# A larger fixed part per float32r matmul in the costs of a hand-written list schedule (hybrid decoder block)

## The chip, the cores and the metric

The kernel runs on one core of a Trainium2 chip. The core has TensorE (PE in the profile; its weight loads are a row of their own, PEld), VectorE (DVE), ScalarE (ACT), GpSimd (POOL) and SyncE (SP, which here issues the DMAs). The metric is the device time of one execution in microseconds; what is compared is the median of several runs.

## The reference

One decoder block for 256 tokens of width 1024, in float32. Three token mixers run on the same normalised input: NSA attention with 16 heads in 4 groups (compressed, selected and window keys), an mLSTM with 4 heads, and cross-attention to 256 memory tokens with 4 heads. Gates merge them; an output projection and a SwiGLU channel mixer of width 2816 follow, each with its RMS norms and residual.

```python
def reference(x, mem, ...):
    ...
    h = rmsnorm(x, g_pre_mix[l])
    z = h @ w_in[l]
    q_nsa, kv_nsa, g_nsa, qkv_ml, if_ml, o_ml, q_mem, g_merge = jnp.split(z, offsets, axis=-1)
    ...
    y_nsa = (gb[..., 0:1] * o_cmp + gb[..., 1:2] * o_slc + gb[..., 2:3] * o_win).reshape(B, S, NSA_Q)
    ...
    y_ml = (jax.nn.sigmoid(o_ml.astype(jnp.float32)) * h_ml).astype(x.dtype)
    y_mem = memory_xattn(q_mem, mem, g_mem[l], w_mem_kv[l])
    gm = jax.nn.sigmoid(g_merge.reshape(B, S, N_BRANCH, D_MODEL))
    y = (gm[:, :, 0] * (y_nsa @ w_proj_nsa[l]) + gm[:, :, 1] * (y_ml @ w_proj_ml[l])
         + gm[:, :, 2] * (y_mem @ w_proj_mem[l]))
    x = x + rmsnorm(y @ w_out[l], g_post_mix[l])
    h = rmsnorm(x, g_pre_ffn[l])
    gu = h @ w_ffn_in[l]
    gate, up = gu[..., :D_FF], gu[..., D_FF:]
    x = x + rmsnorm((jax.nn.silu(gate) * up) @ w_ffn_down[l], g_post_ffn[l])
```

## The kernel before

**Products.** A float32 operand is split into two float32r parts, high and low (`split`: ScalarE copies to the high part, VectorE subtracts it from the source). A product is three matmuls: high by high, high by low, low by high (`mm3`). The weights come as 162 units of 128 x 1024 floats. For a unit, SP loads `raw` (4 buffers), ScalarE writes `whi` and VectorE `wlo` (4 buffers each), and TensorE uses it in 24 matmuls of 256 columns (features on the partitions, `fmaj`) or 12 of 512 columns (tokens on the partitions, `tmaj`).

**Stages, in program order.** Keys and values of the memory branch (to about 28 us), the first input projections with compressed keys and the gates (to about 70 us), memory attention and the NSA keys and values (to about 102 us), then NSA attention, interleaved with the rest of the input projections and the mLSTM (to about 295 us), merge (to about 342 us), output projection, channel mixer.

**NSA attention.** `nsa_half` handles one of the 4 groups for one half of the 128 + 128 tokens. It does two pairs of heads. For each head, TensorE makes scores `sc` (one PSUM tile for the first half of the tokens, two for the second; the tag "s" has three buffers), VectorE takes three maxima `mx`, and ScalarE three exponentials with their sums (into `pc` and `pp`). Per pair VectorE normalises, TensorE transposes (`ptn`), ScalarE and VectorE split the result (`pTh`, `pTl`), and TensorE multiplies with the values (`pvn`). After each half, `fill` records some of the other tasks, named by the letters of `ORDER`, as many as `FILL` says.

**The order of the work.** Nothing is issued as it is written. `Plan.record` keeps every instruction with the parts of tiles that it reads and writes. `Plan.cost` (line 228) estimates its duration. `Plan.schedule` (line 265) then plays the program in planned time: on every engine, among the instructions whose inputs are ready and whose tiles have a buffer, the one first in the program is next (`later` moves some back). If nothing early in the program is ready, a later one is taken, so dense products of the tasks stand between the steps of the attention. `Plan.issue` (line 370) issues all instructions in the order of their planned starts, and that is the order of each engine's queue on the chip, the DMA queue of SP included. On the chip an engine takes its queue in order: if its next instruction is not ready, the engine waits, whatever stands behind.

Planned times of the other engines, in ns: ScalarE 50 (source or result in PSUM) or 95, plus 0.833 per element, plus 93 where it also sums or has a per-partition operand; VectorE 67 plus 1.04 per element (0.52 for a few), plus 60 for each per-partition operand. A result is counted as ready for another engine after the producer's latency (PE 257, ACT 202, DVE 188), with 200 more where TensorE is the one that waits (lines 257 to 263).

A matmul's planned cost and weight load (lines 236 to 240):

```python
if op.eng == "PE":
    dtype = op.a[1].dtype
    op.load = 56.0 if dtype == BF16 else 109.0 if dtype == F32R or op.method == "transpose" else 214.0
    rate = 1.2 if op.method == "transpose" else 0.6 if dtype == F32 else 2.4
    return n / rate + 2
```

In the schedule a matmul starts no sooner than the last matmul's start plus its own `load` (line 337), and TensorE is taken again from its start plus its cost. All instructions are issued from line 382, so every row of the profile names that line; groups are told apart by tile.

Of the kernel before, what the change touches and what calls it, by code (L numbers as in the profile page):

```python
# [17 lines left out]
P = 128  # L18
S = 256          # tokens
D = 1024  # L20
KD = D // P      # feature tiles of the model dimension
NH, NG, HPG, DH = 16, 4, 4, 64
# [9 lines left out]

# columns of w_in
C_Q, C_KV, C_G, C_ML, C_IF, C_O, C_QM, C_MG = 0, 1024, 2560, 2608, 4144, 4152, 4664, 5176

# columns of the array of constants
K_ID, K_TRI, K_RV, K_BM, K_M0, K_C1, K_MT, K_END = 0, 128, 256, 257, 261, 533, 549, 677
# columns of the array of gains and small weights
V_PRE, V_MEM, V_PM, V_PF, V_PO, V_CW, V_CB, V_PEK, V_PEV, V_END = 0, 8, 16, 24, 32, 40, 72, 80, 96, 112


# [1 line left out]
class View:  # L43
    """A part of a tile that has no place yet."""

# [53 lines left out]
    def region(self):  # L99
        """First and last partition, and the elements of a partition as bits."""  # L100
        t = self.tile
        key = repr(self.steps)
        if key not in t.regions:
            p = int(self.ix.flat[0]) // t.n
            bits = np.zeros(t.n, bool)
            bits[self.ix[0].ravel() % t.n] = True
            t.regions[key] = (p, p + self.shape[0], int.from_bytes(np.packbits(bits).tobytes(), "big"))
        return t.regions[key]


class Slot:
    """A tile of the plan: its place is chosen when its first instruction is issued."""

# [49 lines left out]
class Plan:  # L163
    """Records the instructions in program order, with what they read and write, and issues them
    in the order of a list schedule: on every engine the ready one that comes first in the
    program. Tiles of a tag get their buffers in program order."""

# [7 lines left out]
    @contextmanager  # L175
    def later(self, n):
        """The instructions inside come as if n places later in the program."""
        self.boost -= n
        yield
        self.boost += n  # L180
# [47 lines left out]
    def cost(op):  # L228
# [7 lines left out]
        if op.eng == "PE":  # L236
            dtype = op.a[1].dtype
            op.load = 56.0 if dtype == BF16 else 109.0 if dtype == F32R or op.method == "transpose" else 214.0
            rate = 1.2 if op.method == "transpose" else 0.6 if dtype == F32 else 2.4
            return n / rate + 2  # L240
        n = max(v.n for v in views)
# [23 lines left out]
    def schedule(self):  # L265
# [10 lines left out]
        def offer(op):  # L276
            """Makes op a candidate if its new tiles can have places; else it waits for the tag."""
            r = op.ready
            for t in op.tiles:
                if t.real is None:  # L280
                    tag = t.tag
                    if tag.next != t.seq or not tag.free:
                        tag.waiting.setdefault(t.seq, []).append(op)
                        return
                    r = max(r, tag.free[0][0])
            avail[op.eng].append((max(r, held(op)), op))

        def held(op):
            """A bank of PSUM serves one engine at a time, and so do the ports that GpSimd shares."""
            ends = [end + self.latency(o, op) for t in op.tiles if t.psum  # L290
                    for e, (o, end) in t.busy.items() if e != op.eng]
            if op.port:
                ends += [end for e, end in port.items() if e != op.eng]
            return max(ends, default=0.0)
# [91 lines left out]
def block_kernel(ctx, tc, order, xN, xT, memT, cst, vec, row, wg, w1, w2, W, out):  # L386
# [16 lines left out]

# [1 line left out]
    cs = one.tile([P, K_M0], F32, name="cs")  # L405
    vc = one.tile([P, V_END], F32, name="vc")
    ident = cs[:, K_ID:K_ID + P]

# [1 line left out]
    def ps_d(shape, name="pd"):  # L410
# [16 lines left out]

# [1 line left out]
    def split(hi, lo, src):  # L429
        ACT.activation(hi, src, AF.Copy)  # L430
        DVE.tensor_sub(lo, src, hi.bitcast(F32))

# [1 line left out]
    ready = {}  # L434
# [27 lines left out]
    def fmaj(out, xs, ks, wu, b0=0, first=True, last=True):  # L462
        """out [128 features, 256] += blocks of a unit (from b0) times the tiles ks of xs."""
        hi, lo = wu
# [5 lines left out]
    def fpair(xs, w, i, ps_new=ps_d):  # L470
        """[128, 2, 256]: the i-th pair of feature tiles of the weights w."""
        ps = ps_new([P, 2, S])
# [4 lines left out]
    def tmaj(xs, *key, n=4, ps_new=ps_d, into=None, last=0):  # L477
        """[128 tokens, 512] for both halves of the tokens, from n units of two feature tiles each; the
        last ones are used for the first half of the tokens before the second."""
        ps = [ps_new([P, 512]) for _ in range(2)]  # L480
# [21 lines left out]

# [1 line left out]
    ones = one.tile([P, P], F32, name="ones")  # L504
# [4 lines left out]
    def warm_up(n):  # L509
        """Products of no use, that bring the tensor engine's clock up while it would wait."""  # L510
        ps = ps_v([P, P], "warm")
# [3 lines left out]
    def colsum(sq):  # L515
        """[128, 2]: per token, the sum of sq [128, 2, 256] over the partitions and the tiles."""
        col = ps_t([P, 2], "col")
# [6 lines left out]
    def bcast(r, ps):  # L524
        """ps [128, 256]: the column r [128, 2] of the tokens, on every row."""
        for tb in range(2):
# [10 lines left out]

# [1 line left out]
    memt = bigt("G", 3, [P, KD, S], F32, "memt")  # L539
# [99 lines left out]
    DVE.tensor_copy(identb, ident)  # L639
    msk = one.tile([P, 416], BF16, name="msk")          # m0 (272), c1 (16), mt (128)  # L640
    DVE.tensor_copy(msk, mraw)
    M0, MC1, MT, MD = msk[:, 0:272], msk[:, 272:288], msk[:, 288:416], msk[:, 0:P]

# [1 line left out]
    w1t = []  # L645
# [25 lines left out]

# [1 line left out]
    pgf = ps_s([P, S], "pgf")  # L673
# [22 lines left out]

    # running sums of logf, and i - sums
    tri = cs[:, K_TRI:K_TRI + P]
# [32 lines left out]

    # columns: selected keys 128-255, 0-127, compressed keys, window keys 0-127, 128-255
    kh = bigt("KK", 2, [P, NG, 528], F32R, "kh")
# [15 lines left out]

# [1 line left out]
    qkm = [bigt("G", 3, [P, 8, S], F32R, f"qkm{i}") for i in range(2)]  # L751
# [21 lines left out]

# [1 line left out]
    on = bigt("C", 1, [P, 2, 1024], F32, "on")  # L775
# [9 lines left out]

# [1 line left out]
    qm = [bigt("qs", 2, [P, 4, S], F32R, f"qm{i}") for i in range(2)]  # L787
# [3 lines left out]

# [1 line left out]
    ymemt = bigt("E", 2, [P, 2, 4, S], F32R, "ymemt")  # L793
    ymem = [ymemt[:, i] for i in range(2)]
    msc = float(P) ** -0.5
    for h2 in range(2):
        pvm = ps_v([P, 2, S], "pvm")
        ptm = [[work.tile([P, 2, S], F32R, tag=f"pT{i}", bufs=2, name="pTm") for i in range(2)] for _ in range(2)]
        for tb in range(2):
# [16 lines left out]
            for hh_ in range(2):  # L816
                DVE.tensor_scalar(p2[:, hh_, :], p2[:, hh_, :], sm[:, hh_:hh_ + 1], None, op0=ALU.mult)
            pt = ps_t([P, 2, 2, P], "ptx")          # m tile, head, t
            for mt in range(2):
# [11 lines left out]

# [1 line left out]
    for br in range(2):  # L833
# [17 lines left out]

# [1 line left out]
    num = on[:, 1, :].rearrange("p (a h d) -> p a h d", a=2, h=4)  # L853
# [65 lines left out]

# [1 line left out]
    gm = [bigt("G", 3, [P, 8, S], F32, f"gm{b}") for b in range(3)]  # L921
# [117 lines left out]

# [1 line left out]
    last_exp = exps[-12:]  # L1041
# [23 lines left out]

# [1 line left out]
    x1 = bigt("C", 1, [P, 2, D], F32, "x1")  # L1067
# [7 lines left out]
    def scaled(name, xs, n, g, z, scale, pre):  # L1075
        """z [128 tokens, 2, 1024]: the products with the units of a name times the gains g and, per token,
        pre; yields per half of the tokens 1/rms of the products times the root of scale."""
        ss = work.tile([P, 2, 2], F32, tag="ss", bufs=2, name="ss")
# [32 lines left out]

# [1 line left out]
    wq = [bigt(tg, n, [P, 2, 1024], F32R, "wq") for tg, n in (("Y", 2), ("Y", 2), ("V", 1), ("E", 2))]  # L1113
# [53 lines left out]
def _layout(inputs):  # L1167
# [8 lines left out]
    units = {}  # L1176

    def blocks(w, cols, k0=0, k1=None):
        """[128, k, cols] of the rows k0..k1 (tiles)."""
        k1 = w.shape[0] // P if k1 is None else k1  # L1180
# [68 lines left out]
def _stream(units, order):  # L1249
    """The units in the order of their use."""  # L1250
    import numpy as np

    return np.stack([units[key] for key in order])
# [24 lines left out]
```

## Time and profile before

| | us |
|---|---|
| median of 3 runs | 562.93 |
| lowest and highest run | 562.88, 563.34 |
| span of the profiled execution | 561.4 |
| ScalarE busy in the span | 334.2 |
| VectorE busy in the span | 404.5 |

The profile is of one execution; its span runs from the first to the last instruction, and no other time of that execution is given. The mean granted TensorE clock was 0.996 of full speed. Matmuls overlap in the records (the next begins while the last still drains), so the spacing of their starts, not their mean duration, is what one costs. In a group's row, the number after "x" is the count, then follow busy time in us, the mean duration in ns, and after the second bar the engine's idle time just before, with what ended it. In the chain of waits each row has start in us, length in us and the run of instructions.

### The profile page before, as it was taken

How to read it: one execution, taken by the hardware profiler on the slowest of the kernel's cores; microseconds unless marked ns; L12 is line 12 of the kernel's file. 1: busy time of each engine (PE TensorE's matmuls, PEld its weight loads, DVE VectorE, ACT ScalarE, POOL GpSimd, SP SyncE). 2: the span in 40 equal slices, each digit the busy share in tenths (PEclk: the TensorE clock that was granted, in tenths of full speed). 3: DMA queues.
4: the chain of work that ended last, by engine and by line, in shares of the span. 5: the costliest groups of instructions: out<-in, count | busy, mean ns of one | idle time of the engine just before them, and what ended most of it. 6: DMA issues, size and time to landing. Idle time of an engine off the chain costs nothing.

```text
span 561.4 us, 10304 instructions
## 1 busy us (share of the span) xinstructions
PE 551.9 (98%) x3964; PEld 516.5 (92%) x3964; DVE 404.5 (72%) x802; ACT 334.2 (60%) x658; POOL 36.0 (6%) x44
## 2 busy tenths in 40 slices
PE   8999999999999999999999999999999999999994
PEld 8899998998989999999999998878999999988883
DVE  4897398598897989987786877865565656654543
ACT  6775677566596858777697444774444444444430
POOL 1110000002002011302111000000000000000000
PEclk9999999999999999999999999999999999999998
DMA  7994327617345253434435655744555545556522
GB/s 246 356 350 154 113 86 228 205 56 238 129 121 180 76 178 124 135 119 160 151 117 158 216 189 188 257 156 123 177 189 183 182 175 179 186 185 191 189 71 75
DMA packets 29281, 95.28 MB, mean 170 GB/s; under 512 B 3376, under 2 KB 6704, under 8 KB 28976
## 3 DMA queue, kind: packets, MB, share of 16 engines
q1 hardware_dynamic: 29232, 94.63, 51.5%
q8 instruction: 31, 0.51, 0.4%
q14 instruction: 18, 0.15, 0.1%
HBM read 92.52 MB, written 1.05 MB: 167 GB/s over the span
## 4 chain that ended last, share of the span: by engine, by line
PE 92%; DMA 3%; ACT 2%; DVE 2%; issue 0%; SPq 0%; DVEq 0%; ACTq 0%
PE pd L382 46%; PE pss L382 23%; PE pnl L382 6%; PE sc L382 3%; PE pvn L382 3%; PE pmm L382 2%; PE ptn L382 2%; DMA memt<-in_memT 2%; PE ph L382 2%; ACT whi L382 1%; DMA raw<-in_W 1%; PE pw L382 1%; PE pn L382 1%; PE pgf L382 1%; PE psm L382 1%; PE pvm L382 1%
## 5 line engine op out<-in xcount | busy, mean ns | idle before, releaser
L382 DVE TENSOR_TENSOR wlo<-raw,whi 128x1024 fp32r<-128x1024 f32 (+1 forms) x161 | 195.4, 1217 | 102.1 <-ACT whi L382 100.7
L382 ACT ACTIVATE whi<-raw 128x1024 fp32r<-128x1024 f32 (+1 forms) x161 | 167.6, 1046 | 164.3 <-issue 72.3
L382 PE MATMUL pd<-hh,whi 128*128 128x256 f32 x416 | 119.7, 288 | 0.3 <-DVE vs L382 0.3
L382 PE MATMUL pd<-hh,wlo 128*128 128x256 f32 x416 | 119.7, 288 | 0.0
L382 PE MATMUL pd<-hl,whi 128*128 128x256 f32 x416 | 119.5, 287 | 0.0
L382 PEld LDWEIGHTS pd<-hh,whi 128*128 128x128 f32 x416 | 79.5, 191 | 0.8 <-DVE vs L382 0.7
L382 PEld LDWEIGHTS pd<-hl,whi 128*128 128x128 f32 x416 | 79.4, 191 | 0.1
L382 PEld LDWEIGHTS pd<-hh,wlo 128*128 128x128 f32 x416 | 79.4, 191 | 0.0
L382 PE MATMUL pss<-xh,wlo 128*128 128x256 f32 x160 | 45.4, 284 | 0.0
L382 PE MATMUL pss<-xl,whi 128*128 128x256 f32 x160 | 45.4, 284 | 0.0
L382 PE MATMUL pss<-xh,whi 128*128 128x256 f32 x160 | 45.4, 283 | 0.0
L382 PE MATMUL pss<-whi,u 128*128 128x512 f32 x132 | 42.4, 392 | 0.0
L382 PE MATMUL pd<-xh,whi 128*128 128x256 f32 x128 | 36.2, 283 | 0.0
L382 PE MATMUL pd<-xl,whi 128*128 128x256 f32 x128 | 36.2, 283 | 0.0
L382 PE MATMUL pd<-xh,wlo 128*128 128x256 f32 x128 | 36.2, 283 | 0.0
L382 PEld LDWEIGHTS pss<-xh,whi 128*128 128x128 f32 x160 | 30.7, 192 | 0.0
L382 PEld LDWEIGHTS pss<-xl,whi 128*128 128x128 f32 x160 | 30.7, 192 | 0.0
L382 PEld LDWEIGHTS pss<-xh,wlo 128*128 128x128 f32 x160 | 30.7, 192 | 0.0
L382 PEld LDWEIGHTS pss<-whi,u 128*128 128x128 f32 x132 | 24.8, 188 | 5.5
L382 ACT ACTIVATE pp<-sc,mx 128x128 f32<-128x128 f32 (+1 forms) x64 | 27.1, 439 | 0.4 <-DVE mx L382 0.3
L382 PE MATMUL pss<-wlo,u 128*128 128x512 f32 x66 | 25.9, 392 | 0.0
L382 DVE TENSOR_REDUCE mx<-sc 128x1 f32<-128x16 f32 (+2 forms) x96 | 22.6, 284 | 3.3 <-PE sc L382 3.0
(306 smaller groups left out, 1243.9 us busy)
## 6 DMA issues: line engine op xcount, KB each, us to landing
raw<-in_W SPq DMA_DIRECT2D x159, 512.0 KB, 3.4
w<-in_w SPq DMA_DIRECT2D x2, 1024.0 KB, 7.0
raw<-in_W SPq DMA_DIRECT2D x6, 256.0 KB, 5.6
xt<-in_xT SPq DMA_DIRECT2D x2, 512.0 KB, 7.6
x<-in_xN SPq DMA_DIRECT2D x2, 512.0 KB, 4.9
out<-z SPq DMA_DIRECT2D x8, 128.0 KB, 2.0
memt<-in_memT SPq DMA_DIRECT2D x6, 128.0 KB, 5.4
wgt<-in_wg SPq DMA_DIRECT2D x1, 512.0 KB, 6.3
```

Of the source, the lines that this page charges most:

```text
L382: op.ins_ = getattr(op.real, op.method)(*map(arg, op.a), **{k: arg(x) for k, x in op.kw.items()})
```

## The change

In the planned cost of a matmul, the fixed part is 13 ns instead of 2 where the operand is float32r and the method is not a transpose. The weight load's figure of 109 ns stays. All other lines of the diff remove comments and docstrings. The recorded instructions, tiles and buffers are the same; the planned starts, and with them the order of the queues, the places of tiles in their buffers and the order in which weight units are stored, follow from the new costs.

```diff
@@ -237,7 +237,7 @@
             dtype = op.a[1].dtype
             op.load = 56.0 if dtype == BF16 else 109.0 if dtype == F32R or op.method == "transpose" else 214.0
             rate = 1.2 if op.method == "transpose" else 0.6 if dtype == F32 else 2.4
-            return n / rate + 2
+            return n / rate + (13 if dtype == F32R and op.method != "transpose" else 2)
         n = max(v.n for v in views)
         psum = any(v.tile.psum for v in views)
         pointers = sum(v.n == 1 for v in op.ins)
```

## The prediction

> **What bounds the kernel now.** I read the page's engine totals first, then the chain of waits, then the stretch from 100 to 295 us with its instructions grouped by form.
>
> ```profile
> span 561.4 us, 10304 instructions
> ...
> PE 551.9 (98%) x3964; PEld 516.5 (92%) x3964; DVE 404.5 (72%) x802; ACT 334.2 (60%) x658; POOL 36.0 (6%) x44
> ```
>
> TensorE is never idle for long, so the end is set by how many matmuls there are and how far apart they start. The chain of waits gives that distance, since there a run of matmuls has a length and a count:
>
> ```profile
> 155.39 0.66 PE ptn L382 x6
> ...
> 163.25 0.76 PE pw L382 x4
> ...
> 180.63 0.64 PE pq L382 x6
> ...
> 187.12 0.97 PE pn L382 x9
> ...
> 236.65 1.02 PE sc L382 x11
> ...
> 395.73 11.52 PE pd L382 x96
> ...
> 543.50 5.44 PE pss L382 x24
> ```
>
> A 256-wide float32r matmul takes 11.52 / 96 = 120.0 ns of TensorE, a 512-wide one 5.44 / 24 = 226.7 ns, a transpose 110 ns. Columns alone, at 2.4 per ns as the plan counts them, are 106.7 and 213.3 ns: the fixed part is 13.3 ns in both. The plan before charges 108.7 ns for 256 columns and, because it also lets no float32r matmul start sooner than 109 ns after the one before (the weight load), runs them 109.0 ns apart. It is 10% fast. The new constant makes it 119.7 and 226.3.
>
> The Trainium skill speaks against the new constant: "TensorE: Matmul & The Clock Gate", section "Back-to-back issue gap", gives N / 2.4 + 2.5 ns for a warm stream, so 109.2 ns for 256 columns, which is the old charge. This trace does not agree, its streams run at 120.0 ns, and the measurement decides.
>
> Where matmuls depend on little, order is worth nothing. From the stretches of the run:
>
> ```profile
> 220.00:240.00 20.00, 20.00 (x172) 19.65 (x170) 19.55 (x52) 15.43 (x49) 4.98 (x4) 1.00 0.32 107
> ```
>
> ```profile
> 400.00:450.00 50.00, 50.00 (x419) 50.00 (x418) 31.38 (x45) 23.21 (x34) 0.00 (x0) 1.00 0.56 185
> ...
> 500.00:540.00 40.00, 40.00 (x175) 32.68 (x174) 19.75 (x19) 16.48 (x19) 0.00 (x0) 1.00 0.56 184
> ```
>
> (Columns after the length: TensorE, weight loads, VectorE, ScalarE, GpSimd, granted clock, DMA share, GB/s.) From 400 us on, TensorE runs 100% with VectorE at 63% or less and the clock at 1.00; DMA is at 0.56. From 220 to 240 us VectorE is at 98% and ScalarE at 77%: only in the attention part, 100 to 295 us, are the other engines near enough to TensorE for the order to matter.
>
> **The room in that part.** Grouped by form over 100 to 295 us, and the tile of the scores:
>
> ```profile
> L382 PE MATMUL pd<-hh,whi 128*128 128x256 f32 x318 | 91.9, 289 | 0.3 <-DVE vs L382 0.3
> ...
> L382 PE MATMUL pd<-hl,whi 128*128 128x256 f32 x317 | 91.3, 288 | 0.0
> ...
> L382 PE MATMUL ptn<-cs,pp 128*128 128x128 f32 x96 | 15.6, 273 | 0.0
> L382 PE MATMUL pd<-whi,hh 128*128 128x512 f32 x34 | 13.5, 398 | 0.0
> ...
> L382 PE MATMUL pd<-whi,hl 128*128 128x512 f32 x34 | 13.4, 393 | 0.0
> L382 PE MATMUL pvn<-pTh,vs 128*128 128x256 f32 x48 | 13.1, 283 | 0.0
> ...
> L382 PE MATMUL pvn<-ce,vcs 128*128 128x256 f32 x28 | 5.6, 283 | 0.0
> ```
>
> ```profile
> L382 PE MATMUL sc<-msk,identb x64: 172/230/293, 111.5 to 283.1; 128*128 128x128 bf16 x32, 128*128 128x272 bf16 x16, 128*128 128x16 bf16 x16
> ...
> L382 PE MATMUL sc<-kh,qs x48: 278/315/397, 111.3 to 282.9; 128*128 128x272 f32 x32, 128*128 128x256 f32 x16
> ...
> L382 PE MATMUL sc<-kl,qs x48: 276/286/367, 111.4 to 283.0; 128*128 128x272 f32 x32, 128*128 128x256 f32 x16
> ```
>
> The mean durations there overlap one another, so I cost by spacing. The three dense 256-wide products are 318 + 317 + 317 = 952, at 120.0 ns 114.2 us; the 512-wide 3 x 34 = 102, at 226.7 ns 23.1; scores 160 at 1.02 / 11 = 93 ns 14.8; values 48 + 48 + 28 = 124 at 120 ns 14.9; transposes 96, with 16 more by the code, at 110 ns 12.3; four mLSTM heads of 0.76 + 0.64 + 0.97 us 9.5. Sum 188.8 of 195 us: **about 6.2 us** is lost to small waits. That is the most a better order can win here.
>
> By the Trainium skill ("Perfetto Trace Analysis", section "Identifying the Most-Contended Engine") weight-load busy time, not matmul busy time, tells the distance from the limit. By it the room would be 561.4 - 516.5 = 44.9 us. The stretch from 500 to 540 us does not agree: loads are busy 32.68 of 40 us while 175 matmuls leave 229 ns each, the spacing of a 512-wide one.
>
> **The change part by part.** No instruction is added, removed or resized, so 3964 matmuls keep their price. What moves is the order: an instruction is placed where the plan thinks its inputs are ready. With matmuls 119.7 instead of 109.0 ns apart, 9% fewer of them are put between a producer and the matmul that needs it. Transposes, bfloat16 and float32 matmuls keep their charge, and float32r ones of 130 columns or fewer stay at the 109 ns load. Whether 9% fewer still suffices depends on how the plan charges the other engines:
>
> ```profile
> L382 ACT ACTIVATE whi<-raw 128x1024 fp32r<-128x1024 f32 x48 | 50.8, 1065 | 36.2 <-PE pd L382 30.3 <-issue 4.1 <-ACT pp L382 1.8
> L382 DVE TENSOR_TENSOR pTl<-ptn,pTh 128x512 fp32r<-128x512 f32 x24 | 15.6, 682 | 3.3 <-ACT pTh L382 3.1
> ...
> L382 ACT ACTIVATE pTh<-ptn 128x512 fp32r<-128x512 f32 x24 | 13.3, 597 | 4.6 <-PE ptn L382 4.6
> ```
>
> ```profile
> 98.61 1.07 ACT whi L382
> ...
> 99.71 1.23 DVE wlo L382
> 100.93 0.61 DVE vs L382
> ...
> 101.59 0.51 PE pd L382 x2
> ```
>
> The plan's formulas give 948, 599 and 476 ns for the three groups: they are 12, 14 and 25% short. Against that stand its latencies: it adds 202 ns from ScalarE to VectorE and 388 ns from VectorE to TensorE (402 from ScalarE); the trace shows 30 ns (99.68 to 99.71) and 50 ns (101.54 to 101.59).
>
> *Single chains: nothing.* From transposes to value products the plan counts 257 + 476 + 202 + 599 + 388 = 1922 ns. Before, that is 17.6 matmuls, 2116 ns of real TensorE; after, 16.1 matmuls, 1927 ns. The real links after the transpose are 597 + 30 + 682 + 50 = 1359 ns; the link from the transposes to ScalarE is not shown by itself, and it may be up to 570 ns before the chain is late. So these steps lose 190 ns of slack and cost 0. If the cover were gone, the price is at most 0.19 us for each of the 24 split blocks, 4.6 us.
>
> *Backlogs: a loss.* Where one engine works through many instructions in a row, the latency margin counts once and the short charges add up. ScalarE's exponentials of one head, in its timeline:
>
> ```profile
> 213.85 0.26 ACT L382 ACTIVATE pc<-sc,mx 128x16 f32<-128x16 f32 x1
> ...
> 214.10 0.47 ACT L382 ACTIVATE pp<-sc,mx 128x256 f32<-128x256 f32 x1
> ...
> 214.54 0.47 ACT L382 ACTIVATE pp<-sc,mx 128x256 f32<-128x256 f32 x1
> ...
> 215.00 0.28 ACT L382 ACTIVATE pc<-sc,mx 128x16 f32<-128x16 f32 x1
> ```
>
> Head to head is 1.15 us; the plan charges 156 + 356 + 356 = 869 ns. The next scores need the PSUM buffers that these free (three, and a head of the later tokens takes two), and the chain of waits around 190 us shows exactly this wait:
>
> ```profile
> 190.49 0.43 ACT pp L382 x3
> ...
> 191.45 0.35 ACT pp L382 x2
> ...
> 192.72 0.60 PE sc L382 x4
> ```
>
> Before, 869 ns are 7.97 matmuls, 957 ns real; after, 7.26, 871 ns. So each such head comes 86 ns earlier than before against a ScalarE that is already late. For a head of the earlier tokens the plan charges 156 + 250 + 250 = 656 ns and the loss is 65 ns. There are 16 heads of each kind: 1.4 + 1.0 = 2.4 us if every head waits (upper bound), half of it, 1.2 us, if the margin of 402 - 50 = 352 ns covers the first two heads of each four (lower bound for this step). I take the middle, **+1.8 us**, since the chain shows the wait at some heads and not at all. By the page's 109.2 ns the same 0.72 matmuls per head would cost 9% less, 1.6 us.
>
> *Nothing elsewhere.* After 295 us TensorE has no waits to shift, apart from the hand-over between the output projection and the channel mixer, whose chain is ScalarE, VectorE and transposes that keep their charge. The first 30 us follow the loads. DMAs keep their order on the SP queue but for weight units fetched a matmul or so later; at a DMA share of 0.32 to 0.56 that costs 0.
>
> Sum: 561.4 + 1.8 = 563.2 us of span; the runs' median of 562.93 lies 1.5 us above the span, so **564.7 us**.
>
> **Rivals.** *Faster.* ScalarE stood 30.3 us of this part ahead of `whi<-raw`, waiting for TensorE to give back a weight buffer (the row above), with exponentials queued behind. The plan thought a unit of 24 matmuls took 2.62 us, really 2.88. Charged right, such splits are placed later, exponentials pass them, and part of the 6.2 us comes back: half is 559.8 us, all 556.7. It decides once exponentials leave ScalarE more than 86 ns per head earlier. Against it: the short charges on ScalarE and VectorE remain and were roughly matched by TensorE's.
>
> *No change.* The slack in most chains swallows 9%, and the few late ones trade places: 562.9 us.
>
> *Clearly slower.* VectorE at 19.55 of 20 us has no reserve. If each of the four pairs of half passes catches one 1.27 us split (1.23 in the chain row) ahead of a reduction that TensorE waits for, 4 x 1.25 = 5.0 us join the 1.8: 569.7 us. For it: VectorE's charge is 14% short while TensorE's no longer is. Against it: VectorE is at 63% or less elsewhere and the splits have four buffers.
>
> **How the numbers follow.** Forecast 0.36 (its own range 563.8 to 566.0), faster 0.32, no change 0.17, clearly slower 0.15. A measurement of this kernel tells about 0.2%, 1.1 us, from no change: faster 0.32, same 0.17, slower 0.51. The range from 559.5 to 570.5 holds half or more of the faster case and nearly all of the slower ones; it leaves out about 0.17.
>
> **What would show it.** Right: dense 256-wide spacing still 120.0 ns; from 400 us on the same stretches, shifted; between 100 and 295 us the same matmuls over some 197 us; more time of scores waiting for ScalarE. Wrong: ScalarE's 30.3 us shrinks and the attention part gets shorter (faster rival), VectorE reaches 100% in several stretches there (clearly slower), or the time moves in the first 100 us or the hand-over at 350 us, where I expect nothing.

## The result and the profile after

| | before | after |
|---|---|---|
| median (lowest to highest; 4 runs each, side by side) | 563.13 us (562.88 to 563.34) | 572.02 us (570.79 to 572.9) |
| ratio, 95% interval | | 1.0152 (1.0135 to 1.0169) |
| span of the profiled execution | 561.4 us | 571.1 us |

The changed order is 8.9 us slower. The sign was forecast; the size was not (564.7, with 570.5 as the upper end). Two executions further down, the profiled ones of e1_after_exp (1893.69 us) and k17_early_exp (3049.52 us), were in a slow state, so they are left out of the medians and these two kernels have no figures by stage. The page of after, its totals and the shares of its chain of waits by engine:

```profile
span 571.1 us, 10314 instructions
...
PE 557.3 (98%) x3964; PEld 517.7 (91%) x3964; DVE 406.4 (71%) x802; ACT 335.2 (59%) x658; POOL 35.4 (6%) x44
...
PE 81%; DVE 8%; ACT 6%; DMA 2%; issue 2%; SPq 0%; DVEq 0%; ACTq 0%
```

The same 3964 matmuls are there. On the chain, VectorE and ScalarE now hold 14% of the span (before, the line begins "PE 92%; DMA 3%; ACT 2%; DVE 2%"). TensorE is still "98% busy": outside its busy time it has 9.5 us before and 13.8 us after, 4.3 us more where the span grew by 9.7, so this number hides over half of the loss. The number of matmuls per stretch shows it. Stretches of after (columns as in the prediction):

```profile
200.00:250.00 50.00, 49.10 (x405) 46.90 (x404) 42.22 (x115) 35.50 (x98) 7.21 (x6) 1.00 0.39 138
...
400.00:450.00 50.00, 50.00 (x420) 50.00 (x418) 31.24 (x44) 23.78 (x35) 0.00 (x0) 1.00 0.50 181
```

And the one of before that was not shown yet:

```profile
200.00:250.00 50.00, 50.00 (x422) 48.64 (x421) 45.71 (x125) 37.60 (x105) 7.03 (x6) 1.00 0.45 147
```

Between 200 and 250 us after runs 405 matmuls where before runs 422: 17 fewer, 2.0 us at 120.0 ns, with only 0.90 us of idle time in the row. VectorE is less busy than before, not full. From 400 us on nothing differs but the shift.

The shift itself is found by numbering the matmuls by start time, which works for any order since all kernels have the same 3964. The time from one numbered start to the next gives the length of a stage (the first is counted from the start of the span):

| stage, by matmul number | before, us | after | difference |
|---|---|---|---|
| 1: 0 to 700 (until about 102 us) | 101.59 | 103.31 | +1.72 |
| 2: 700 to 1000 | 41.54 | 41.81 | +0.27 |
| 3: 1000 to 2200 (most of the attention) | 149.52 | 154.16 | +4.64 |
| 4: 2200 to 2600 (merge) | 47.78 | 47.77 | -0.01 |
| 5: 2600 to 2900 (output projection, hand-over to the mixer) | 57.06 | 60.11 | +3.05 |
| 6: 2900 to the start of the last | 156.51 | 156.51 | 0 |

The differences add up to 9.67 us, that of the two spans; from the last start to the end it is 7.4 us in both. So there are three places, of which the prediction had named one, and priced it at 1.8.

### The profile page after: what moved, and what is told of

It is laid out like the page before. It is cut to its first block, busy times and chain, and to the rows that moved or that the text cites. A ratio compares the mean times of both kernels' runs of the same rounds, so it can differ in the third digit from the quotient of the medians.

```text
span 571.1 us, 10314 instructions
## 1 busy us (share of the span) xinstructions
PE 557.3 (98%) x3964; PEld 517.7 (91%) x3964; DVE 406.4 (71%) x802; ACT 335.2 (59%) x658; POOL 35.4 (6%) x44
## 3 DMA queue, kind: packets, MB, share of 16 engines
q1 hardware_dynamic: 29232, 94.63, 47.5%
## 4 chain that ended last, share of the span: by engine, by line
PE 81%; DVE 8%; ACT 6%; DMA 2%; issue 2%; SPq 0%; DVEq 0%; ACTq 0%
PE pd L382 39%; PE pss L382 23%; PE pnl L382 6%; PE pvn L382 2%; ACT pp L382 2%; DVE wlo L382 2%; PE pmm L382 2%; PE sc L382 2%; DMA raw<-in_W 2%; PE ph L382 2%; PE ptn L382 1%; ACT whi L382 1%; ACT pc L382 1%; DVE mx L382 1%; DVE pp L382 1%
```

## Three theories

**A, covered lateness.** Some instructions of ScalarE and VectorE take longer than the plan charges. Before, the plan's TensorE ran 9% fast, which gave real time to all of them; the new constant takes that away. **B, any other order loses.** The order before happened to be good, and every change of charges gives a worse one. **C, lost distance alone.** 9% fewer matmuls between a producer and its consumer cost time whatever the other charges are.

**What is really undercharged.** Charges in the plan are spacings: an engine is taken again after the charge. Held against starts in the trace, not durations, most are exact. ScalarE in the timeline of before:

```profile
350.78 1.06 ACT L382 ACTIVATE whi<-raw 128x1024 fp32r<-128x1024 f32 x1 [1.66 <-PE pss L382]
351.75 1.04 ACT L382 ACTIVATE wq<-raw 128x1024 fp32r<-128x1024 f32 x1
```

A 1024-wide copy is 1.06 us long, but the next starts 0.97 us after it; the plan says 948 ns. By the same reading, the median over all neighbours without a wait between them: `whi` 965 ns, `pTh` 478 (plan 476), `wlo` 1142 (1132), `pTl` 601 (599). The Trainium skill says so too: "ScalarE: Activation LUTs", section "What ACT_TABLE_LOAD costs", has activations back to back overlap by about 93 ns. The trace agrees, with 1065 - 965 = 100 ns.

Two kinds are short. First, the exponentials, which have a per-partition bias and also accumulate: 450, 343 and 250 ns apart for 256, 128 and 16 columns, where the plan says 356, 250 and 156. It adds 93 ns once, whether one or both apply; they take it twice. There are 96 in the attention and 8 in memory attention. Second, instructions on 64 partitions with an operand in PSUM. Timeline of before, VectorE and ScalarE:

```profile
49.69 1.73 DVE L382 COPY st<-pd 64x255 f32<-64x255 f32 x4 [1.03 <-PE pd L382]
...
51.51 1.56 ACT L382 ACTIVATE st<-pd 64x256 f32<-64x256 f32 x4 [0.83 <-DVE st L382]
```

That is 433 and 390 ns each, where the plan says 332 and 263; `qs` takes 700 (599), `yT` 423 (333), each ahead of another of its kind. It is not a fixed price of the instruction: on ScalarE, ahead of an instruction on 128 partitions that does not wait, the same trace has `st` at 284 ns (263), `qs` at 481 and `ylo` at 506 (both 476).

**What it does in after.** ScalarE's timeline at one half pass of earlier tokens:

```profile
224.56 0.27 ACT L382 ACTIVATE pc<-sc,mx 128x16 f32<-128x16 f32 x1 [0.35 <-DVE mx L382]
...
225.51 0.28 ACT L382 ACTIVATE pc<-sc,mx 128x16 f32<-128x16 f32 x1
...
226.45 0.30 ACT L382 ACTIVATE pc<-sc,mx 128x16 f32<-128x16 f32 x1
```

From head to head it is 0.95 us, while the plan says 0.656: 0.29 us, three times 93 ns and a little. After four heads, 12 exponentials, ScalarE is by this count 12 x 93 ns = 1.1 us behind the plan (an estimate), and the queue's order does not change for that: `whi` and `ylo` stand behind them. The chain of waits of after, from there on:

```profile
224.56 0.36 ACT pc L382 x2
224.93 0.70 ACT pp L382 x4
...
228.27 0.70 ACT pp L382 x4
228.97 0.47 ACT whi L382
...
229.94 0.60 ACT ylo L382
...
230.57 0.42 DVE yT L382
...
231.56 0.36 PE pvn L382
```

The chain stays off TensorE for 7 us and runs through the exponentials to `pvn`, where TensorE waits (waits of TensorE and ScalarE in after, 100 to 299 us; total, times and longest):

```profile
PE pvn L382 <- DVE yT L382: 0.6, 1, 0.6
...
ACT whi L382 <- PE pd L382: 29.9, 23, 2.7
```

That is one place. Most of the waiting lies in TensorE's weight loads. Their waits before (100 to 295 us):

```profile
PEld sc L382 <- ACT pp L382: 1.3, 5, 0.5
```

and after (100 to 299 us):

```profile
PEld sc L382 <- ACT pp L382: 2.9, 10, 0.5
PEld pvn L382 <- ACT pTh L382: 1.0, 2, 0.8
...
PEld ptn L382 <- DVE pp L382: 0.9, 2, 0.6
...
PEld ptc L382 <- DVE pTl L382: 0.5, 2, 0.3
```

The scores wait 1.6 us more for exponentials. The other three waits, 2.4 us together, were not there before: value products and transposes that wait for what comes behind the exponentials. Together it is 4.0 of the 4.9 us that stages 2 and 3 lost.

Before, a half pass of some 24 us (195 / 8) lasted 9% or about 2.1 us longer than planned (an estimate from the matmuls' spacing), and most of the 1.1 us of lateness went into that unseen, as far as the waits show. With TensorE charged as it runs, this cover is gone.

## The experiments

`Plan.FIX` is the fixed part of a float32r matmul in all kernels below (2 before, 13 after). Where it varies, it is set anew at the places in `block_kernel` that stand for a stage, so it holds for the matmuls recorded from there on:

```diff
-            return n / rate + 2
+            return n / rate + (Plan.FIX if dtype == F32R and op.method != "transpose" else 2)
...
+    Plan.FIX = ...     # start: before the attention
     ...
+    Plan.FIX = ...     # attention and what is interleaved with it
     gm = [bigt("G", 3, [P, 8, S], F32, f"gm{b}") for b in range(3)]
     ...
+    Plan.FIX = ...     # output projection and later
     x1 = bigt("C", 1, [P, 2, D], F32, "x1")
```

The right charge for exponentials ("exp" below) is

```diff
-            return (50 if psum else 95) + 0.833 * n + 93 * ("accum_out" in op.kw or pointers > 0)
+            both = "accum_out" in op.kw and sum(v.n == 1 for v in op.ins) > 0
+            return (50 if psum else 95) + 0.833 * n + 93 * ("accum_out" in op.kw or pointers > 0) + 93 * both
```

All runs in one table. "2/13/2" gives the fixed part in the three places. The last columns are the differences from before, in us, of stages 1, 2, 3 and 5 of the table above (4 and 6 are within 0.07 everywhere); they come from one execution each, the profiled one. Stage 1 varies between executions of kernels that are alike up to there: -0.61 to +0.16 with 2 ns and the old charges, +1.10 to +2.35 with 13.

| run | fixed part | other charges | median (range) | ratio (95%) | 1 | 2 | 3 | 5 |
|---|---|---|---|---|---|---|---|---|
| e3_early13 | 13/13/2 | | 569.93 (569.51-570.65) | 1.0109-1.0139 | +1.10 | +0.26 | +4.62 | +0.37 |
| e2_late13 | 2/2/13 | | 565.47 (564.3-569.55) | 1.0029-1.0079 | +0.16 | -0.01 | -0.05 | +2.17 |
| w13 | 2/13/2 | | 568.02 (567.93-568.76) | 1.0069-1.0099 | -0.61 | +0.26 | +4.82 | +0.35 |
| first13 | 13/2/2 | | 565.68 (565.3-565.99) | 1.0024-1.0052 | +2.35 | -0.01 | +0.01 | +0.11 |
| n13 | 2/13/2 | exp | 564.22 (563.63-565.08) | 1.0007-1.0026 | -0.34 | +1.46 | -0.52 | +0.39 |
| n17 | 2/17/2 | exp | 564.19 (563.85-568.12) | 1.001-1.004 | -0.03 | -0.16 | +1.20 | +0.35 |
| e1_after_exp | 13/13/13 | exp | 568.44 (565.96-569.41) | 1.0058-1.0116 | | | | |
| e1b_after_exp | 13/13/13 | exp | 569.36 (566.83-571.34) | 1.0091-1.0158 | +0.86 | +1.49 | -0.59 | +1.86 |
| e4_before_exp | 2/2/2 | exp | 561.45 (560.48-561.79) | 0.9958-0.9982 | -0.81 | +0.02 | -1.97 | -0.01 |
| e5_13_all | 13/13/13 | exp, two VectorE forms | 568.53 (567.2-569.75) | 1.0077-1.0117 | +2.15 | +3.16 | -0.95 | +1.68 |
| e6_13_early_all | 13/13/2 | exp, two VectorE forms | 565.67 (564.61-566.63) | 1.0029-1.0064 | +1.06 | +1.68 | -1.01 | +0.02 |
| k17_early_exp | 17/17/2 | exp | 566.06 (565.63-566.92) | 1.0036-1.0063 | | | | |
| c5_wrong_exp | 5/5/5 | | 566.84 (565.78-569.23) | 1.0044-1.0086 | -0.11 | +0.21 | +1.30 | +3.23 |
| c20_wrong_exp | 20/20/20 | | 577.25 (575.17-581.18) | 1.0198-1.0303 | +7.36 | +0.99 | +5.95 | +3.66 |
| h1_x1_first | 2/2/13 | one order fixed | 564.14 (563.6-565.43) | 1.0015-1.0033 | -0.25 | -0.02 | -0.06 | +1.07 |
| h2_as_before | 2/2/13 | two orders fixed | 562.65 (562.24-565.32) | 0.9977-1.001 | -0.59 | -0.02 | -0.08 | -0.01 |
| first13_own | 13/2/2 | exp and all 64-partition, first place only | 564.3 (562.98-564.88) | 1.0001-1.0023 | +0.37 | -0.05 | -0.06 | -0.03 |
| all2_charges | 2/2/2 | exp and all 64-partition | 561.28 (560.69-561.73) | 0.9954-0.9979 | +0.32 | +0.03 | -1.91 | -0.01 |

e1b_after_exp is e1_after_exp again, for its trace. Some of these executions had the granted clock at half for a while: c20_wrong_exp for 6.8 us in stage 1 (from 47.5 us) and 3.4 us in stage 5, e5_13_all for 3.4 us in stage 2 (from 140 us), after and c5_wrong_exp for 3.4 us in stage 5. Half of such a stretch at most is time lost to the clock in its cell. The kernel before, beside each batch, had medians of 562.86 to 563.26.

### Which part of the program pays

> The fixed part is 13 ns only for matmuls recorded from the output projection on, 2 ns before. Place of the loss: by the two traces the hand-over between output projection and channel mixer costs 3.0 us of the 9.7. If that loss is made there, this kernel takes about 566 us (563.1 + 3.0) with a stall at the first gate products; if it is inherited from the order of the work before, about 563 us.

> The fixed part is 13 ns for matmuls recorded ahead of the output projection, 2 ns from there on. If the losses of the parts add up: 563.1 + 6.6 = 569.7 us, with the hand-over as before the change. If the hand-over's loss comes from the order before it: 572 us.

The loss splits: the constant ahead of the output projection gives stages 1 to 3, the constant from there on gives stage 5. Two more runs split the first part.

> 13 ns only for matmuls recorded in the attention stage (with the tasks between its parts), 2 ns before and after it, exponentials charged as in the kernel before. Theory A: this stage alone loses its 4.6 us: 567 to 568 us, the first 700 matmuls and everything after the 2200th as in the kernel before. If the loss was handed on from the first 100 us, 564 us or less.

> 13 ns only ahead of the attention stage. By the changed kernel's trace the first 700 matmuls lose 1.7 us, by the one with 13 ns up to the projection 1.1 us: 564 to 565 us, with nothing more lost after the 1000th matmul.

Used in the attention alone, the constant gives all of stage 3 (+4.82 against +4.64 in after) and nothing else of size; used ahead of it, stage 1 alone (its +2.35 holds a wait of 0.8 us at 23 us, `col` for a square of the first loads, which among these executions only e5_13_all shares). The three parts add up: 565.68, 568.02 and 565.47 less the medians beside them are 2.51 + 4.85 + 2.45 = 9.8 us; after is 8.9.

### The attention: is it the exponentials' charge?

> The changed kernel, but an exponential that both takes a per-partition bias and accumulates its sum is charged 93 ns more in the plan (before the change's trace its starts lie 450, 343 and 250 ns apart at 256, 128 and 16 columns; the plan has 356, 250 and 156). Theory A (the plan's only wrong charge was the exponentials', hidden while matmuls were charged 10% too little; correcting the matmuls alone exposed it): the attention part gives back most of its 5 us, the scores' and transposes' waits shrink, 565 to 568 us if the hand-over still costs 3 us. Theory B (any other order than the one that stood loses, whatever the charges): no better than 570 us. Theory C (the lost 9% of distance is what matters, since the plan's order leaves each consumer just its planned latency): 570 to 573 us.

> The changed kernel with each exponential that takes a bias and accumulates charged 93 ns more, as before, for a profile of it. Theory A (the exponentials' missing charge, exposed by the correct matmul charge, makes the attention part late): the 100 to 297 us part loses 2 us or less against the kernel before instead of 4.9, the hand-over still loses some 2 to 3 us, 566 to 569 us in all. Theory C (9% less distance between producer and consumer costs by itself): the part still loses 4 us or more.

> The kernel before (fixed part 2 ns) with the exponentials charged 93 ns more. Theory A: ScalarE's charges matter by their ratio to TensorE's; here TensorE's are 10% short and ScalarE's right, so consumers are placed later than needed: 560 to 563 us. Theory B: 566 us or more, as for any new order. Theory C: at or below 563 us, since the distances of before stay or grow.

With the exponentials charged right, stage 3 goes from +4.64 to -0.59, as A says. C, lost distance alone, falls as the main cause: behind every other instruction the distances are as short as in after. With 2 ns and right exponentials the kernel is faster than before, by 1.97 us in stage 3 and 1.6 in the median: that is against B, as a new order won. In its trace (100 to 295 us) no weight load of a score waits for an exponential, where before had 1.3 us of that: the short charge cost time before the change, too, and the cover was not whole. But the medians of e1_after_exp and e1b_after_exp lie just above A's ranges, e1b_after_exp is still 6.5 us slower than before, and stage 2, +0.27 in after, is +1.49. Its stages explain 3.7 us; they are of its fastest execution (566.83 us, mean granted clock 0.996), and two of its four (571.09 and 571.34) had 0.990. The same comparison without the other places is cleaner:

> As w13, but exponentials that take a bias and accumulate are charged 93 ns more. Theory A: from the 1000th to the 2200th matmul it is 0.5 us or more faster than the kernel before; a stall of 1.8 us that the plan itself has at the mLSTM's values stays: 563 to 565 us in all. Theory C: 567 us or more.

w13 and n13 differ in the exponentials' charge alone: stage 3 +4.82 and -0.52. Chain of waits, the same stretch of both; first w13:

```profile
222.24 0.37 ACT pc L382 x2
222.60 0.70 ACT pp L382 x4
...
226.66 0.47 ACT whi L382
...
229.25 0.36 PE pvn L382
```

then n13:

```profile
221.25 0.71 ACT pp L383 x4
...
222.00 0.65 PE sc L383 x3
222.65 2.98 PE pd L383 x25
...
230.18 0.47 PE pvn L383 x4
```

In w13 the chain is the one of after, 7 us through ScalarE and then VectorE; in n13 it is back on TensorE after the first head. Of the four waits of weight loads above, n13 has one left (100 to 295 us):

```profile
PEld sc L383 <- ACT pp L383: 0.6, 2, 0.3
```

The waits of `pvn`, `ptn` and `ptc` are gone with it, though the charges of their own chains are as in w13. So those chains were late because of the exponentials ahead of them.

**Stage 2.** The rise in n13, e1b_after_exp, e5_13_all and e6_13_early_all is one wait. TensorE's waits of e1b_after_exp, 130 to 140 us:

```profile
PE pd L383 <- DVE vml L383: 1.8, 1, 1.8
```

It is not lateness: the plan of that kernel has the same idle time of TensorE, 1.93 us, at that place (2.45 in e5_13_all, which waits 2.0). Both PSUM buffers of dense products are then held for `vml` of the mLSTM. The list schedule looks no further than what is ready, and it ran into that with these charges and not with others (n17: -0.16).

**Other values of the constant.** The load's 109 ns is the floor, so 2, 5, 13, 17 and 20 mean 109, 111.7, 119.7, 123.7 and 126.7 ns for 256 columns.

> Fixed part 5 ns, the exponentials charged as before; its plan leaves no idle time in the attention part either. Theory A: the same stretch loses about 3/11 of 4.65 us, 1.3 us, and the hand-over, whose order in the plan is that of the changed kernel, 2 to 3 us: 566 to 568 us. Theory B: the attention part loses as much as at 13 ns or nothing.

> Fixed part 20 ns for every float32r matmul, the exponentials charged as before. Its plan leaves TensorE no idle time in the attention part (0.0 us; the changed kernel's 0.3). Theory A (missing charges of the exponentials, met 9% earlier at 13 ns, 15% earlier at 20): the attention part from the 1000th to the 2200th matmul loses more than the changed kernel's 4.65 us, some 6 to 8 us; 573 us or more in all. Theory B (the order's accidents): anything between a gain and a loss, no relation to the constant.

> Exponentials charged 93 ns more, a fixed part of 17 ns ahead of the output projection and 2 from there on: the plan keeps 0.2 us of idle TensorE in the attention part, where 13 ns with the same charges had 1.8 us in one stall. Theory A: with right charges a larger matmul charge costs nothing by itself, so the attention part is as fast as in the kernel before or faster, 561 to 563.5 us. Theory C (distance lost is time lost): 567 us or more.

> As n13, with 17 ns: the plan then has 0.2 us of idle TensorE in the stage. Theory A: 560.5 to 563 us, and the 566.2 us with 17 ns from the start on were lost in the first 100 us. If the attention stage itself loses with 17 ns: 565 us or more, and right charges for the exponentials alone aren't enough there.

With the old charge of exponentials, stage 3 rises steadily, 0, +1.30, +4.64, +5.95: it grows at every step, with no value of the margin that is free. With the right one it is -1.97, -0.52, +1.20 for 2, 13 and 17. n17 was a miss: I had expected 560.5 to 563 us, and margin beyond the true 120.0 ns to be harmless. k17_early_exp missed A's range, too (566.06 against 561 to 563.5); by n17, some 2 us of that lie ahead of the attention. So even with right exponentials stage 3 loses 1.4 us from 2 to 13. Is that the other short charges?

> The changed kernel with the exponentials charged 93 ns more and VectorE's two-source instructions that read PSUM on 64 partitions 95 ns more (query split, sums of the attention's halves: starts 700 and 423 ns apart against 599 and 333 in the plan). Theory A: the attention part is no slower than in the kernel before; only the hand-over's 2 to 3 us is left, 564 to 566 us. Theory C: the part still loses 3 us or more, 568 us or more.

> As the last one, but the fixed part is 2 ns from the output projection on, so that the hand-over has the order of the kernel before. Theory A: 560 to 563 us, at or below the kernel before. Theory C: 566 us or more. The hand-over loses 0.5 us or less against the kernel before in either.

```diff
+            half = psum and op.outs[0].shape[0] == 64 and op.method in ("scalar_tensor_tensor", "tensor_add")
-            return 67 + (0.52 if fast else 1.04) * n + 60 * pointers
+            return 67 + (0.52 if fast else 1.04) * n + 60 * pointers + 95 * half
```

Also a miss. Charging these forms moves stage 3 only from -0.59 to -0.95 and -1.01. In e5_13_all stages 1 and 2 are longer, but they hold the wait for the first loads (1.0 us) and the stretch at half clock; e6_13_early_all, without these, has +1.06 and +1.68. **Open:** about 1 us of stage 3 that depends on the matmuls' charge with the known short charges mended. C (distance) or an accident of order can both be its cause; no run here tells them apart.

### The hand-over from output projection to mixer

No exponentials run here, and e2_late13 has +2.17 with 13 ns from here on only. Timelines of before, VectorE, then TensorE:

```profile
360.56 1.23 DVE L382 TENSOR_TENSOR wq<-raw,wq 128x1024 fp32r<-128x1024 f32 x1 [0.18 <-ACT wq L382]
361.71 1.41 DVE L382 SCALAR_TENSOR_TENSOR x<-z,ss,x 128x512 f32<-128x512 f32 x2
363.03 1.22 DVE L382 TENSOR_TENSOR wlo<-raw,whi 128x1024 fp32r<-128x1024 f32 x1
```

```profile
365.33 0.74 PE L382 MATMUL pd<-wq,xh 128*128 128x512 f32 x2 [0.16 <-ACT xh L382]
```

and of after, ScalarE, VectorE, TensorE:

```profile
368.00 1.06 ACT L382 ACTIVATE whi<-raw 128x1024 fp32r<-128x1024 f32 x1 [1.07 <-DMA raw<-in_W]
...
371.29 1.06 ACT L382 ACTIVATE whi<-raw 128x1024 fp32r<-128x1024 f32 x1 [0.78 <-DMA raw<-in_W]
```

```profile
369.10 1.23 DVE L382 TENSOR_TENSOR wlo<-raw,whi 128x1024 fp32r<-128x1024 f32 x1 [1.61 <-ACT whi L382]
370.24 1.41 DVE L382 SCALAR_TENSOR_TENSOR x<-z,ss,x 128x512 f32<-128x512 f32 x2
```

```profile
373.69 1.15 PE L382 MATMUL pd<-wq,xh 128*128 128x512 f32 x2 [1.33 <-ACT xh L382]
```

The residual sums `x<-z,ss,x` stand on the path to `xh`, the mixer's input. Before, VectorE does them and then the split `wlo`. After, `wlo` stands ahead: it waits for `whi`, which waits 1.07 us for its load, and the sums wait behind both. A further `whi`, waiting 0.78 us for its load, stands ahead of the squares of `x` on ScalarE. The new plan has TensorE idle for 2.05 us at this place where the old has 1.04. In e2_late13 TensorE's waits are (342 to 402 us):

```profile
PE pd L382 <- ACT xh L382: 0.8, 1, 0.8
PE ptx L382 <- DVE x L382: 0.6, 1, 0.6
PE pd L382 <- DVE xl L382: 0.5, 1, 0.5
```

1.9 us; before, the 0.16 of the row above is the only one. To test that it is the order, the charge of 13 ns was kept and the order put back by added dependences, first of VectorE's splits on the sums, then also of the splits from the third unit on, on the first half's `xh` and `xl`. In the cut, `first` holds the sums and `kept` the last `xh` and `xl` of the first half; `hold` is filled while the second product is recorded. Against the order of e2_late13, h1_x1_first moves one `wlo` and puts squares of `x` ahead of one `whi`; h2_as_before moves two `wlo`, one `whi` and two matmuls.

```diff
     def split(hi, lo, src):
-        ACT.activation(hi, src, AF.Copy)
-        DVE.tensor_sub(lo, src, hi.bitcast(F32))
+        late = kept[:2] if hold and seen[0] > 1 else []      # h2_as_before only
+        seen[0] += bool(hold)                                # h2_as_before only
+        ACT.activation(hi, src, AF.Copy, after=late)         # h2_as_before only
+        DVE.tensor_sub(lo, src, hi.bitcast(F32), after=late or hold[:2])
     ...
+    hold += first     # the two sums of the first half
     up0 = tmaj((xh, xl), "ffn_up", ps_new=ps_ds)
+    hold.clear()
```

> 13 ns from the output projection on alone (565.5 us when it ran), with one order undone: VectorE's low parts of the first weights of the mixer's second product come after the first two residual sums. If the hand-over's loss is that the residual sum stands behind a low part that waits for a weight load (wlo behind whi behind the DMA), this kernel takes 563 to 564 us. If the loss has another cause (DMA bandwidth, the clock's dip by itself), it stays at 565 us or more.

> 13 ns from the output projection on, with two orders undone: the low part that stood ahead of the residual sums, and the third weight split that stood ahead of the normalised input's parts (xh, xl). If the hand-over's loss is this order alone, the hand-over costs within 0.3 us of the kernel before and the kernel takes 562.8 to 563.4 us; if part of it comes from later transfers, 564 us or more.

+2.17 becomes +1.07 and then -0.01, and the median 565.47, 564.14, 562.65. So the misplaced splits are the whole of this part, an order that the planner chose; 1.0 us of the loss is idle time in its own plan.

After has 0.9 us more there than e2_late13. Its wait is shorter, 1.33 us in all; but the clock (the column ahead of the last two, in the windows of after) was not granted in full behind that wait:

```profile
373.00:375.00 2.00, 1.30 (x3) 1.09 (x4) 2.00 (x5) 2.00 (x9) 0.00 (x0) 0.70 0.49 162
375.00:377.00 2.00, 2.00 (x6) 1.54 (x5) 1.67 (x8) 1.97 (x5) 0.25 (x1) 0.50 0.93 291
```

Six 512-wide matmuls in 2 us, where 226.7 ns each would give nearly nine. With 1.2 us at half in the first row, 2.0 in the second and 0.2 behind them (0.95 from 377 to 379 us) it is 3.4 us, so at most 1.7 us lost. The executions with such a stretch here have +3.05, +3.23 and +3.66 in stage 5 (after, c5_wrong_exp, c20_wrong_exp), those of 13 ns without it +1.68 to +2.17. After's four runs spread with their mean granted clock: 572.9 and 572.55 us at 0.995, 571.5 at 0.997, 570.79 at 0.998.

### The first 100 us, and all charges mended

> As the kernel with 13 ns ahead of the attention stage alone (565.7 us), with that stage's short charges corrected too: 93 ns more for an exponential with bias and sum, 120 (ScalarE) and 100 (VectorE) more for an instruction on 64 partitions that reads or writes PSUM (starts 390 and 433 ns apart against 263 and 332 in the plan). If the first 100 us lose for the same reason as the attention stage, the first 700 matmuls take at most 0.5 us more than in the kernel before, 562.7 to 563.9 us. If they lose for another reason, 565 us or more.

```diff
-            return (50 if psum else 95) + 0.833 * n + 93 * ("accum_out" in op.kw or pointers > 0)
+            return (50 if psum else 95) + 0.833 * n + 93 * ("accum_out" in op.kw or pointers > 0) + 93 * both + 120 * (psum and op.outs[0].shape[0] == 64)
...
-            return 67 + (0.52 if fast else 1.04) * n + 60 * pointers
+            return 67 + (0.52 if fast else 1.04) * n + 60 * pointers + 100 * half
```

(`half` is now any VectorE instruction on 64 partitions with PSUM.) Stage 1 goes from +2.35 to +0.37 in the profiled executions, but the median only from 565.68 to 564.3, between the two ranges expected: of 2.5 us over the kernel before beside it, 1.1 are left. So the short charges are a good part of the loss in stage 1, not shown to be all of it. Chain of waits at memory attention, first13:

```profile
83.09 0.91 ACT pp L382 x4
...
88.27 0.84 DVE wlo L382
...
89.41 0.69 DVE ymemt L382
...
90.24 0.36 PE pvm L382
```

and first13_own:

```profile
84.90 0.96 PE pd L384 x8
85.86 1.30 PE pvm L384 x11
87.16 4.06 PE pd L384 x32
```

The same picture as in the attention: with the charges mended the chain at this place is TensorE's alone. The last run leaves the matmuls at 2 ns and mends the rest:

> The kernel before (2 ns throughout) with the same three charges corrected for the whole program: 560 to 562 us, as the one with the exponentials alone (561.45), if the 64-partition charges matter little at 2 ns; below 560 us if they matter as well.

561.28 us, 1.9 less than before beside it (ratio 0.9966, 0.9954 to 0.9979). It is the best of all versions and beats both kernels, though it is within the spread of e4_before_exp (561.45).

## Why the prediction was right in sign and wrong in size

**Right.** Dense matmuls are still 120.0 ns apart. From 400 us on the same stretches came, shifted: stage 6 is 156.51 us in both. The mechanism, undercharged exponentials that lose their cover, was the one of "Backlogs: a loss", and w13 against n13 shows it. The sign of a faster rival, ScalarE's 30.3 us of waiting for weight buffers shrinking, did not come (29.9). The prediction holds the 120.0 ns against the formula in the Trainium skill, "TensorE: Matmul & The Clock Gate", section "Back-to-back issue gap"; that section of the Trainium skill calls it the gap of an isolated matmul and has 131 ns at 512 columns for a stream of loads and matmuls. The 120.0 and 226.7 ns here agree with neither, and no term of the sum rests on the formula.

**The step that failed: "Single chains: nothing".** The steps from transposes to value products were put at nothing ("lose 190 ns of slack and cost 0"), and waits of the transposes themselves are in no term; in after the weight loads of both wait 2.4 us, where before had none of these waits. The step costed each chain as if ScalarE were free when the transposes are done. But on ScalarE its instructions stand in one queue behind the exponentials, and these were late by their full shortfall, 93 ns each, three a head, 279 ns, not by the 65 to 86 ns that I counted as lost: the 9% was lost over the whole half pass, about 2.1 us. n13 shows that it is this lateness and not the chains' shorter distance: with the exponentials mended the waits are gone. My own row had the shortfall: head to head 1.15 us against 869 ns charged, 281 ns. I read it as "already late" and priced only the change.

**The term that came out near, partly by luck.** The +1.8 us for scores that wait for exponentials is 2.9 - 1.3 = 1.6 us by the loads' waits. But it is not 86 ns at about half of the heads: the places of such waits went from 5 to 10, some 0.3 us each.

**A reading that failed.** "They are 12, 14 and 25% short" compared durations with charges. I had warned of just this for matmuls, and did it for ScalarE and VectorE: by spacing, these three groups are charged to about 2%. So I took VectorE for short as well, and the rival "clearly slower" rested on that. Its 569.7 us was the nearest number, but its mechanism did not happen: VectorE did not fill, it was at 42.22 of 50 us where the loss is.

**"Nothing elsewhere" failed twice.** Stage 1 lost 1.72 us, in good part by the mechanism that I had confined to the attention; memory attention's exponentials and the 64-partition forms are short there too (which of the two weighs more was not tried). The hand-over lost 3.05, of which 1.2 (after's wait) to 2.2 (e2_late13) are order and most of the rest the clock in that execution. I had argued that its chain keeps its charges. It does, but the splits of the next weight units compete with it on ScalarE and VectorE, and when these are placed follows from the matmuls' charge.

**Distance by itself.** In n13 the shorter distances cost no time in stage 3 against before; against e4_before_exp they may cost up to 1.4 us, which is open.

**Of the rivals,** "faster" was wrong for 13 ns, but its idea, charges that are right let the order win back some of the 6.2 us, came true in the other place: mending the exponentials alone won 1.97 us in stage 3.

## What to carry to other kernels

A planner's charge is to be held against the distance from start to start, for every engine, before one of them is mended. Where a plan was tuned by time, one wrong charge may be paying for another; a correct constant for the busiest engine takes away the margin that hid the rest, and what comes into the open can be the whole of the other errors, not the percentage by which the margin shrank, and it shows at whatever stands behind the late instructions in their queue. Then mend the small ones first, and look for places where the plan itself now idles: 2.2 us at the hand-over, and 1.5 us at 136 us in the kernels with mended exponentials, were order that the planner chose, not lateness.

## What was not expected of the hardware

An exponential with a per-partition bias that also accumulates starts the next one 93 ns later than one addition of 93 ns explains (450 against 356 ns at 256 columns); the trace shows the sum's part as an instruction of its own, ACTIVATION_READ_ACCUMULATOR, with 93 ns to the next start. Instructions on 64 partitions with an operand in PSUM, one behind another, started 90 to 127 ns further apart than the formula that fits those on 128; ahead of an instruction on 128 partitions three ScalarE ones came within 30 ns of it. What decides this was not tried.

After a wait of 1.33 us in a stream that was otherwise dense, the granted clock fell to 0.50 for 3.4 us (0.70, 0.50 and 0.95 in the three rows of 2 us from 373 to 379 us in after; 0.78, 0.50 and 0.86 from 368 to 374 in c5_wrong_exp). It stayed at 1.00 behind e1b_after_exp's wait of 1.8 us at 136 us, but not behind the wait of 2.0 us at the same place in e5_13_all (0.54 and 0.60 from 140 to 144 us, again 3.4 us at half). The Trainium skill, "TensorE: Matmul & The Clock Gate", section "What's actually happening", says that the clock falls to half after an idle window of about 3.4 us and that the window runs freely. The half is what the trace shows; here 1.33 us without matmuls came before it at one place, and 1.8 us at another had no such effect; what decides between them was not tried.
